# Small vector work handed from GpSimd to VectorE, and conditioning and cached values loaded at other places, in a two-layer diffusion step

## The chip, the cores and the metric

The kernel runs on one core of one Trainium2 chip. A core has TensorE (PE in the profile: matrix products and transposes, with PEld for its weight loads), VectorE (DVE), ScalarE (ACT), GpSimd (POOL) and SyncE (SP), which here issues nearly all DMAs. Each engine runs its own instructions in order and waits on the others by semaphores. The metric is the device time of one execution in microseconds (us): 1993.41, the median of three runs.

## The reference

One inference step of a backbone with two layers over 256 context tokens and 1024 latent tokens, model width 1024, all in float32. Layer 0 mixes tokens with differential attention (8 heads, two score maps of width 64 each, values of width 128), layer 1 with multi-head latent attention. Around both stands the same frame:

```python
sh, sc, gt = silu(cond) @ w_ada[i] + b_ada[i]            # conditioning, one vector for context, one for latent
h  = rmsnorm(x, g_pre[i]) * (1 + sc) + sh
x  = x + gt * rmsnorm(mixer(h) @ w_out[i], g_post[i])

# layer 0, differential attention
q, k, v, gate = split(h @ w_in)                          # q and k of latent tokens get a rotary embedding
p  = softmax(q k^T / 8)                                  # two maps per head; latent: 1024 keys and 256 cached
w  = p[0] - lam * p[1]
o  = rmsnorm(w @ v, g_sub) * (1 - lam_init)
y  = o * silu(gate)                                      # then y @ w_out
```

The outputs are both updated token streams and the layers' states (keys and values of layer 0, compressed latents and positional keys of layer 1).

## The kernel before

**Precision.** Float32 products are made of three products of a rounded type: each operand is split into a high part and the rest, a low part, and `mm3` (L324 to L329) adds high x high, high x low, low x high. So everything that goes into a product costs a cast (the high part) and a subtraction (the low part). For a weight, `weights` (L304 to L322) takes two 128-row blocks at a time: a DMA into a buffer "wst" (three of them turn round, `bufs=3`), ScalarE's cast into "wh", and the subtraction into "wl" on L320, which GpSimd does, or GpSimd and VectorE in turn where `lo_engs=self.LO` is given (output products, layer 1's projections).

**Tokens.** The 1280 tokens are handled as five pairs of 128-row tiles: latent pairs 0 to 3 and the context pair 4 (`CTXP`). `norm_pair` (L257) sums squares on ScalarE, forms the reciprocal root on GpSimd (`rstd`, L248: a scaling on L251, a power on L253), and scales x on VectorE. `norm_pair_to_hT` (L280) transposes x on TensorE; ScalarE applies scale and shift of the conditioning into "hfull" (L297), VectorE copies the high part, and VectorE or GpSimd by a fixed list subtracts the low part (L299).

**The start.** `constants` (L119) brings both conditioning vectors, the four norm gains and the biases of both layers (96 rows of 128) into one tile "rb", transposes it with the identity (L134) and forms silu of the conditioning. `run` (L1494 on) then loads in this order on SP's queue: first piece of w_ada, x of pair 0, first weights of V, x of pairs 1 to 3, the other pieces. In this stage the order on TensorE is the order of the code: conditioning sums, then 12 products of zeros with the identity (`WARM`), then the norms and products of V of head pair 0, pair by pair.

**Layer 0.** Work items of fixed order ("k0 q0 k1 q1 ..." and then "v1 a0 a1 v2 g0 ...": keys, queries, values, gates of a head pair, and conditioning sums) are chained: an item's weights are loaded before the item in front of it ends (`chain`, and `yield None` in an item). The first string fills 60 to 360 us. From 360 to 960 us the second is fed in small portions, by planned costs, between the attention of the 8 heads: scores, maximum (VectorE, L605), its combination (L613, L614) and the exponential (ScalarE, L617), the weighted difference of the two maps (L648 on VectorE, its factor on L643), its transposes and their splitting (L671 to L674), and `l0_values` (L678), which ends with the norm over a head's output y. There the squares are summed on ScalarE, the power and its combination with the softmax sum are formed on GpSimd, and y is scaled (L707); 40 such pairs of scalings in all. An item of values has the cached values of its head pair to split too, ahead of its second token pair (`l0_cached_v`, L509: a load into a staging buffer "s", then a split). Rows of q and k go out to DRAM and come back in another layout ("qsd", "ksd"), again by SP.

**From 960 us.** `y_chunk` (L743) loads 256 columns of y and of the gate, multiplies them on GpSimd (L757), transposes and splits. `out_items` (L929) multiplies by w_out and sums squares, `residual` (L976) adds x, and three queues of deferred work (`Later`, with the distances `HD`, `HE`, `ND` in steps) put late y chunks, norms and transposes of layer 1's input between the products. From 1200 us layer 1 runs, and from 1800 us its output product, with the same `residual` at the very end.

**What sets the order.** Apart from the hand-ordered stretch at the start, a scheduler orders each engine's instructions by the code's order and its own estimates; buffers turn round in pools of a fixed number.

## Time and profile before

| what | value |
|---|---|
| time, median of 3 runs | 1993.41 us (1992.21 to 1994.4) |
| time of the profiled execution | 1997.65 us |
| its span in the trace | 1995.8 us |
| mean granted clock of TensorE | 0.989 |
| TensorE busy | 1911.7 us, 96% of the span |
| VectorE busy | 1248.4 us, 63% |
| ScalarE busy | 963.9 us, 48% |
| GpSimd busy | 498.9 us, 25% |
| moved by DMA | 237.66 MB, 119 GB/s over the span |

The span runs from the first to the last recorded instruction; the execution's own time has 1.85 us more around it. Shares of busy time are means over stages with different limits, so a table by stage is the thing to read first, then what TensorE waits for. A row of a group names the line, the engine, the operation, output and inputs with their shape, the count, then busy microseconds and mean nanoseconds of one, and behind the second bar how long the engine stood before these instructions and what ended most of that.

### The profile page before, as it was taken

The numbers are of one execution on the slowest core, as the hardware profiler recorded it, in microseconds if no ns is written. First come the engines' busy times: TensorE is split into PE (matmuls) and PEld (weight loads), VectorE is DVE, ScalarE is ACT, GpSimd is POOL, SyncE is SP. The second block draws the span as 40 slices with busy tenths as digits, with TensorE's granted clock in tenths as the row PEclk, the third lists the DMA queues.
The fourth block names the chain that finished last, engine by engine and source line by source line (L and its number), as shares of the span: only waits on it lengthen the run. The fifth ranks groups of instructions, "written<-read, shape, count | busy, mean of one in ns | idle before, by whom it ended". The sixth has DMA issues, their size and how long they took to land.

```text
span 1995.8 us, 36154 instructions
## 1 busy us (share of the span) xinstructions
PE 1911.7 (96%) x13468; PEld 1721.9 (86%) x13468; DVE 1248.4 (63%) x2461; ACT 963.9 (48%) x2409; POOL 498.9 (25%) x693
## 2 busy tenths in 40 slices
PE   6999999999999999999998999999999999999998
PEld 5788888798989787988898999889899999998998
DVE  4644446788878786888427533446667767777413
ACT  4422123667666665666435533335445554455421
POOL 3354443213121212224334442100000000004214
PEclk9999999999999999999998999999999999999999
DMA  8555544544455454455624312442110111113412
GB/s 307 170 169 175 188 157 137 157 138 132 128 147 162 129 165 127 133 148 180 194 98 135 97 51 62 145 135 60 42 36 28 47 39 50 38 38 96 160 56 106
DMA packets 225009, 237.66 MB, mean 119 GB/s; under 512 B 25313, under 2 KB 192577, under 8 KB 224705
## 3 DMA queue, kind: packets, MB, share of 16 engines
q1 hardware_dynamic: 224672, 235.29, 38.3%
q8 instruction: 107, 1.75, 0.4%
q14 instruction: 70, 0.57, 0.1%
q10 hardware_dynamic: 160, 0.05, 0.0%
HBM read 160.48 MB, written 74.78 MB: 118 GB/s over the span
## 4 chain that ended last, share of the span: by engine, by line
PE 43%; DVE 5%; POOL 3%; ACT 2%; issue 2%; DMA 2%; SPq 0%; POOLq 0%; ACTq 0%; DVEq 0%
PE pj L327 7%; PE pj L329 7%; PE pj L328 7%; PE tp L671 3%; PE tp L327 3%; PE tp L328 3%; PE tp L329 3%; PE S L1280 1%; PE S L1281 1%; PE S L1278 1%; PE S L1279 1%; PE S L1277 1%; PE S L603 1%; DVE ptl L674 1%; DMA yst<-yTd 1%
## 5 line engine op out<-in xcount | busy, mean ns | idle before, releaser
L327 PE MATMUL pj<-wh,hh 128*128 128x256 f32 (+1 forms) x1264 | 369.4, 292 | 6.6 <-DVE ptl L674 3.5
L328 PE MATMUL pj<-wl,hh 128*128 128x256 f32 (+1 forms) x1264 | 359.1, 284 | 6.1 <-DVE wl L320 3.7
L329 PE MATMUL pj<-wh,hl 128*128 128x256 f32 (+1 forms) x1264 | 358.8, 284 | 3.4 <-POOL hl L299 1.7
L320 POOL TENSOR_TENSOR wl<-wst,wh 128x512 fp32r<-128x512 f32 (+3 forms) x95 | 110.7, 1173 | 655.1 <-ACT wh L319 608.9
L327 PEld LDWEIGHTS pj<-wh,hh 128*128 128x128 f32 x1264 | 241.7, 191 | 11.7 <-DVE ptl L674 4.1
L328 PEld LDWEIGHTS pj<-wl,hh 128*128 128x128 f32 x1264 | 242.2, 192 | 8.3 <-DVE wl L320 4.1
L329 PEld LDWEIGHTS pj<-wh,hl 128*128 128x128 f32 x1264 | 241.7, 191 | 6.5 <-POOL hl L299 3.1
L329 PE MATMUL pj<-hh,wl 128*128 128x512 f32 (+1 forms) x512 | 188.5, 368 | 1.0 <-POOL wl L365 0.9
L327 PE MATMUL pj<-hh,wh 128*128 128x512 f32 (+1 forms) x512 | 188.3, 368 | 0.0
L328 PE MATMUL pj<-hl,wh 128*128 128x512 f32 (+1 forms) x512 | 187.8, 367 | 0.0
L605 DVE TENSOR_REDUCE mA<-S 128x1 f32<-128x1024 f32 x128 | 155.4, 1219 | 46.8 <-PE S L603 45.9
L617 ACT ACTIVATE e<-S,bias 128x1024 f32<-128x1024 f32 x128 | 142.9, 1117 | 81.6 <-DVE bias L614 81.4
L603 PE MATMUL S<-kl,q 128*128 128x512 f32 x512 | 150.4, 414 | 5.5 <-ACT e L617 5.1
L673 ACT CAST pth<-tp 128x512 fp32r<-128x512 f32 (+1 forms) x208 | 98.4, 511 | 83.0 <-PE tp L671 81.9
L673 ACT CAST pth<-pj 128x512 fp32r<-128x512 f32 (+1 forms) x192 | 98.4, 519 | 73.4 <-PE pj L671 70.8
L674 DVE TENSOR_TENSOR ptl<-tp,pth 128x512 fp32r<-128x512 f32 (+1 forms) x208 | 115.1, 580 | 14.1 <-ACT pth L673 13.3
L648 DVE SCALAR_TENSOR_TENSOR e<-e,cf,e 128x512 f32<-128x512 f32 (+1 forms) x192 | 121.4, 674 | 1.1
L674 DVE TENSOR_TENSOR ptl<-pj,pth 128x512 fp32r<-128x512 f32 (+1 forms) x192 | 113.0, 592 | 12.1 <-ACT pth L673 11.5
L329 PEld LDWEIGHTS pj<-hh,wl 128*128 128x128 f32 x512 | 96.3, 188 | 20.9 <-POOL wl L365 3.9
L328 PEld LDWEIGHTS pj<-hl,wh 128*128 128x128 f32 x512 | 96.3, 188 | 16.9
L319 ACT CAST wh<-wst 128x512 fp32r<-128x512 f32 (+3 forms) x136 | 76.7, 574 | 70.1 <-issue 24.9
L603 PEld LDWEIGHTS S<-kl,q 128*128 128x128 f32 x512 | 88.8, 192 | 25.1 <-ACT e L617 8.1
(323 smaller groups left out, 5247.7 us busy)
## 6 DMA issues: line engine op xcount, KB each, us to landing
q<-qsd SPq DMA_DIRECT2D x320, 64.0 KB, 2.1
wst<-in_da_w_in_dram SPq DMA_DIRECT2D x64, 256.0 KB, 3.5
kl<-ksd SPq DMA_DIRECT2D x64, 192.0 KB, 3.7
wst<-in_w_out_dram SPq DMA_DIRECT2D x48, 256.0 KB, 2.9
ast<-in_w_ada_dram SPq DMA_DIRECT2D x8, 1024.0 KB, 6.3
wh<-in_w_ada_dram SPq DMA_DIRECT2D x32, 256.0 KB, 4.2
wl<-in_w_ada_dram SPq DMA_DIRECT2D x32, 256.0 KB, 5.1
vdh<-s SPq DMA_DIRECT2D x24, 256.0 KB, 2.1
```

Source lines behind the costliest of these rows:

```text
L319: nc.scalar.copy(wh, st)
L320: (lo_engs or [nc.gpsimd])[k0 // kb % len(lo_engs or [0])].tensor_tensor(out=wl, in0=st, in1=f32(wh), op=ALU.subtract)
L327: nc.tensor.matmul(out, a[0], b[0], start=first, stop=False)
L328: nc.tensor.matmul(out, a[0], b[1], start=False, stop=False)
L329: nc.tensor.matmul(out, a[1], b[0], start=False, stop=last)
L603: nc.tensor.matmul(S[:, so:so + 512], st(cc, o), kl[cc][:, so:so + 512], start=(o == 0), stop=(o == 1))
L605: nc.vector.reduce_max(out=mA[:, cc:cc + 1], in_=S, axis=AX.X)
L617: nc.scalar.activation(u.es[cc][:, 0:1024], A[cc], AF.Exp, bias=bias[:, cc:cc + 1], scale=0.125, accum_out=u.zA[:, cc:cc + 1])
L648: nc.vector.scalar_tensor_tensor(out=w[:, sl], in0=w[:, sl], scalar=cf, in1=e0[:, sl], op0=ALU.mult, op1=ALU.add)
L671: nc.tensor.transpose(tp[:, j, :], u.e[:, (c0 + j) * P:(c0 + j + 1) * P], self.ident)
L673: nc.scalar.copy(hi, tp[:, 0:cn, :])
L674: nc.vector.tensor_tensor(out=u.ptl[g][:, 0:cn, u.i * P:(u.i + 1) * P], in0=tp[:, 0:cn, :], in1=f32(hi), op=ALU.subtract)
```

## The change

Nothing of what is computed changes. Five things are done elsewhere or at another time:

1. **Low parts on VectorE.** `weights` always subtracts on VectorE (the list of engines is gone), and so does `norm_pair_to_hT`. The low parts that `weights_x` makes for keys and queries stay on GpSimd, as do the rotations there.
2. **Scalings and sums on VectorE.** The scaling in `rstd`, the sums of squares in `norm_pair` and `out_items`, the product of y and gate, and the additions of `residual`. The power of a reciprocal root stays on GpSimd. In `l0_values` the factor is no longer formed by itself: one instruction scales y by both factors.
3. **Conditioning in a tile of its own.** The two conditioning vectors come into a tile "rc" of 16 rows and are transposed alone; gains and biases come into "rb" of 80 rows, which is transposed behind the conditioning sums, in `ada_bias`.
4. **Order at the start.** The DMA of pair 0's x goes ahead of the first piece of w_ada. Of the 12 products of zeros, 8 stand ahead of the conditioning sums and 4 behind.
5. **Cached values with the weights.** They are loaded by the item's `load`, into one of the three "wst" buffers, ahead of the item's four weight pieces; the split stays where it was.

GpSimd's instructions fall from 698 to 266, VectorE's rise from 2463 to 2816, TensorE's from 13294 to 13295.

```diff
-    WARM = 12
+    WARM = 8
...
     def constants(self, cp, tmp, ps):
         nc, I = self.nc, self.I
-        rb = self.t(tmp, [96, P], "rb")
-        vecs = [I["c"][0], I["c_ctx"], I["g_pre"][0], I["g_pre"][1], I["g_post"][0], I["g_post"][1]]
+        rc = self.t(tmp, [16, P], "rc")
+        for i, v in enumerate([I["c"][0], I["c_ctx"]]):
+            nc.scalar.dma_start(rc[8 * i:8 * i + 8, :], v.rearrange("(a p) -> a p", p=P))
+        rb = self.t(tmp, [80, P], "rb")
+        vecs = [I["g_pre"][0], I["g_pre"][1], I["g_post"][0], I["g_post"][1]]
...
-        nc.tensor.transpose(pt[:, 0:96], rb, self.ident[:96, :96])
-        self.cols = self.t(cp, [P, 12, 8], "cols")
-        nc.vector.tensor_copy(self.cols, pt[:, 0:96].rearrange("p (a b) -> p a b", b=8))
+        nc.tensor.transpose(pt[:, 0:16], rc, self.ident[:16, :16])
+        ccol = self.t(cp, [P, 2, 8], "ccol")
+        nc.vector.tensor_copy(ccol, pt[:, 0:16].rearrange("p (a b) -> p a b", b=8))
...
-    def ada_bias(self, pool):
+    def ada_bias(self, cp, pool):
         nc = self.nc
+        pt = self.t(self.c.pj, [P, 512], "pj")
+        nc.tensor.transpose(pt[:, 0:80], self.rb, self.ident[:80, :80])
+        self.cols = self.t(cp, [P, 10, 8], "cols")
+        nc.vector.tensor_copy(self.cols, pt[:, 0:80].rearrange("p (a b) -> p a b", b=8))
...
     def rstd(self, pool, ss, n, width=1, tag="rs"):
-        nc.gpsimd.tensor_scalar(out=v, in0=ss, scalar1=1.0 / n, scalar2=EPS, op0=ALU.mult, op1=ALU.add)
+        nc.vector.tensor_scalar(out=v, in0=ss, scalar1=1.0 / n, scalar2=EPS, op0=ALU.mult, op1=ALU.add)
...
-            nc.gpsimd.tensor_tensor(out=ss[:, 0, :], in0=ss[:, 0, :], in1=ss[:, 1, :], op=ALU.add)
+            nc.vector.tensor_tensor(out=ss[:, 0, :], in0=ss[:, 0, :], in1=ss[:, 1, :], op=ALU.add)
...
-                (nc.vector if k in (self.HL if l else (1, 3, 5, 7)) else nc.gpsimd).tensor_tensor(out=hl[:, k, :], in0=full, in1=f32(hh[:, k, :]),
-                                                              op=ALU.subtract)
+                nc.vector.tensor_tensor(out=hl[:, k, :], in0=full, in1=f32(hh[:, k, :]), op=ALU.subtract)
...
             nc.scalar.copy(wh, st)
-            (lo_engs or [nc.gpsimd])[k0 // kb % len(lo_engs or [0])].tensor_tensor(out=wl, in0=st, in1=f32(wh), op=ALU.subtract)
+            nc.vector.tensor_tensor(out=wl, in0=st, in1=f32(wh), op=ALU.subtract)
...
+        def load():
+            cr = self.l0_load_cached_v(hp) if kind == "v" else None
+            return self.weights(W, [((2048 if kind == "v" else 3072) + hp * 256, 256)]), cr
+
+        def gen(ld):
+            ws, cr = ld
...
                 if kind == "v" and pr == 1:
-                    self.l0_cached_v(hp)
+                    self.l0_split_v(hp, cr, 8)
...
-    def l0_cached_v(self, hp):
-        cr = self.t(self.c.stg, [P, 2, 256], "s")
+    def l0_load_cached_v(self, hp):
+        cr = self.t(self.wp, [P, 2, 256], "wst", bufs=3)
         self.nc.sync.dma_start(cr, self.I["cache_diff_v"][0, 0, :, 2 * hp:2 * hp + 2].rearrange(
             "(t p) h d -> p t (h d)", p=P))
-        self.l0_split_v(hp, cr, 8)
+        return cr
...
         r = self.rstd(c.st, ss, P, 2, tag="ors")
         for i in range(2):
-            f = self.t(c.st, [P, 1], "of")
-            nc.gpsimd.tensor_tensor(out=f, in0=r[:, i:i + 1], in1=rz[i], op=ALU.mult)
-            nc.gpsimd.tensor_scalar(out=y[:, i, :], in0=y[:, i, :], scalar1=f, scalar2=None, op0=ALU.mult)
+            nc.vector.tensor_scalar(out=y[:, i, :], in0=y[:, i, :], scalar1=r[:, i:i + 1], scalar2=rz[i],
+                                    op0=ALU.mult, op1=ALU.mult)
...
-        nc.gpsimd.tensor_tensor(out=y, in0=y, in1=g, op=ALU.mult)
+        nc.vector.tensor_tensor(out=y, in0=y, in1=g, op=ALU.mult)
...
-            nc.gpsimd.tensor_tensor(out=xt[:, i, :], in0=xt[:, i, :], in1=tmp, op=ALU.add)
+            nc.vector.tensor_tensor(out=xt[:, i, :], in0=xt[:, i, :], in1=tmp, op=ALU.add)
...
-                nc.gpsimd.tensor_tensor(out=z[:, i, :], in0=z[:, i, :], in1=x0[i], op=ALU.add)
+                nc.vector.tensor_tensor(out=z[:, i, :], in0=z[:, i, :], in1=x0[i], op=ALU.add)
...
+            load_x(0)
             load_ada(0)
-            self.ada_bias(self.ac)
-            load_x(0)
             load_v(0)
...
             load_x(4)
+            cached = self.l0_load_cached_v(0)
             with tc.manual_schedule(engines={mybir.EngineType.PE}):
-                m = ada_sums(0)
                 idle = self.t(ps, [P, 512], "xt")
                 for _ in range(self.WARM):
                     nc.tensor.matmul(idle, self.identr, self.zeros, start=True, stop=True)
+                m = ada_sums(0)
+                for _ in range(self.WARM // 2):
+                    nc.tensor.matmul(idle, self.identr, self.zeros, start=True, stop=True)
+                self.ada_bias(cp, self.ac)
                 ada_cols(0, m)
```

The scheduler puts the moved instructions at new places. Each row below has the line, the operation, output and inputs (with the numbers of their buffers) and the shape; line numbers behind the change are up to 13 higher.

The first place is VectorE at the very start: "identr" is the identity that every transpose and the products of zeros need, "ss" and "rsv" belong to the norm of the first x. Before:

```order
L129 CAST identr_227<-idt_222 128x128
L147 TENSOR_REDUCE sel_242<-idt_222 128x2
L136 COPY cols_233<-pj_231 128x96
L140 TENSOR_SCALAR cc_237<-cols_233 128x16
L181 COPY bias_141_254<-cols_233 128x48
L183 TENSOR_SCALAR bias_141_254<-cols_233 128x8 x2
L144 SCALAR_TENSOR_TENSOR silc_239<-th_235,cc_237 128x2x8
L270 TENSOR_SCALAR x_258<-x_258,rs_363 128x1024
```

With the change:

```order
L258 TENSOR_SCALAR rsv_368<-ss_363 128x2
L131 CAST identr_228<-idt_223 128x128
L149 TENSOR_REDUCE sel_243<-idt_223 128x2
L138 COPY ccol_234<-pj_232 128x16
L277 TENSOR_SCALAR x_251<-x_251,rs_370 128x1024
L142 TENSOR_SCALAR cc_238<-ccol_234 128x16
L277 TENSOR_SCALAR x_252<-x_252,rs_370 128x1024
L146 SCALAR_TENSOR_TENSOR silc_240<-th_236,cc_238 128x2x8
L326 TENSOR_TENSOR wl_260<-wst_261,wh_259 128x512
L1479 COPY m_173_341<-ad_324 128x512
```

The scaling of the first norm's sum (rsv) now stands ahead of the identity's cast, and a low part of V's weights (L326) ahead of the copy of the conditioning sums (L1479).

The second place is the norm over y in layer 0's attention ("oss" and "ors" are its sum and its power, "ptl" the low part of transposed weights). Before, on GpSimd, behind three low parts of the item's weights:

```order
L320 TENSOR_TENSOR wl_3036<-wst_3037,wh_3035 128x512
L320 TENSOR_TENSOR wl_3042<-wst_3043,wh_3041 128x512
L320 TENSOR_TENSOR wl_3048<-wst_3049,wh_3047 128x512
L251 TENSOR_SCALAR orsv_3663<-oss_3576 128x2
L253 TENSOR_TENSOR ors_3665<-orsv_3663,mhalf_229 128x2
L706 TENSOR_TENSOR of_3667<-ors_3665,rz_3307 128x1
L706 TENSOR_TENSOR of_3670<-ors_3665,rz_3423 128x1
L707 TENSOR_SCALAR y_3575<-y_3575,of_3667 128x128
L707 TENSOR_SCALAR y_3575<-y_3575,of_3670 128x128
```

With the change, on VectorE, behind one of the first heads' units:

```order
L624 TENSOR_TENSOR m_4458<-m_4458,mA_4461 128x2
L654 SCALAR_TENSOR_TENSOR cf_4527<-Z_4339,neglam_1091,rz_4525 128x1
L625 SCALAR_TENSOR_TENSOR bias_4459<-m_4458,negl_1097 128x2
L258 TENSOR_SCALAR orsv_4534<-oss_4437 128x2
L659 SCALAR_TENSOR_TENSOR e_4377<-e_4377,cf_4527,e_4376 128x512 x2
L659 SCALAR_TENSOR_TENSOR e_4377<-e_4377,cf_4527,e_4376 128x256
L716 TENSOR_SCALAR y_4436<-y_4436,ors_4536,rz_4159 128x128
L716 TENSOR_SCALAR y_4436<-y_4436,ors_4536,rz_4282 128x128
L616 TENSOR_REDUCE mA_4583<-S_4585 128x1
L685 TENSOR_TENSOR ptl_934_4455<-pj_4591,pth_931_4452 128x4x128
```

The sum's scaling (L258) and y's (L716) now stand between the bias and the weighted difference of one unit and the maxima of another; GpSimd's power, not in this row, lies between the two.

The third place is SP's queue where the weights of the first item of values ("v1") are loaded, while the last queries are still being written. Before:

```order
L457 DMA out_dram<-s_2859 128x2x256
L317 DMA wst_3031<-in_da_w_in_dram 128x2x256
L388 DMA ksd_116_184<-hi_2882 128x256
L388 DMA ksd_116_184<-lo_2883 128x256
L388 DMA ksd_116_184<-hi_2888 128x256
L388 DMA ksd_116_184<-lo_2889 128x256
L317 DMA wst_3037<-in_da_w_in_dram 128x2x256
L317 DMA wst_3043<-in_da_w_in_dram 128x2x256
L317 DMA wst_3049<-in_da_w_in_dram 128x2x256
L388 DMA qsd_112_180<-hi_2943 128x512
L388 DMA qsd_112_180<-lo_2944 128x512
```

With the change:

```order
L463 DMA out_dram<-s_2864 128x2x256
L522 DMA wst_3034<-in_cache_diff_v_dram 128x2x256
L394 DMA ksd_116_184<-hi_2887 128x256
L394 DMA ksd_116_184<-lo_2888 128x256
L394 DMA ksd_116_184<-hi_2893 128x256
L394 DMA ksd_116_184<-lo_2894 128x256
L323 DMA wst_3038<-in_da_w_in_dram 128x2x256
L323 DMA wst_3044<-in_da_w_in_dram 128x2x256
L323 DMA wst_3050<-in_da_w_in_dram 128x2x256
L394 DMA qsd_112_180<-hi_2948 128x512
L394 DMA qsd_112_180<-lo_2949 128x512
```

The cached values (L522) have the place of the item's first weight piece. The other three take the places of the three behind it, and the fourth piece, wst_3056, stands nine rows behind wst_3050, past all eight qsd writes of 128x512, where before it had gone out ahead of them.

37 lines of the change are left out of this document (18 added, 19 removed).

## The prediction

> **What bounds the kernel now.** I read the page's busy times first, then a table of busy time by stage, then what TensorE waits for, then the groups of GpSimd and VectorE, whose work changes hands.
>
> ```profile
> PE 1911.7 (96%) x13468; PEld 1721.9 (86%) x13468; DVE 1248.4 (63%) x2461; ACT 963.9 (48%) x2409; POOL 498.9 (25%) x693
> ```
>
> TensorE is busy for 96% of the span, so at most 84 us could ever be won by taking waits away, and VectorE has 37% free on average. The average hides the stages; the next table has one row each, with the columns PE, PEld, DVE, ACT, POOL, granted clock, DMA share and GB/s.
>
> ```profile
> 0.00:60.00 60.00, 43.17 (x345) 34.80 (x349) 30.18 (x66) 27.04 (x51) 21.21 (x37) 0.94 0.76 260
> 200.00:360.00 160.00, 156.11 (x895) 134.68 (x896) 87.51 (x135) 46.83 (x106) 61.94 (x55) 0.99 0.48 156
> 360.00:780.00 420.00, 408.41 (x2910) 355.64 (x2909) 332.34 (x662) 271.26 (x716) 94.84 (x178) 0.99 0.50 146
> 780.00:960.00 180.00, 170.91 (x1264) 154.51 (x1264) 157.71 (x299) 123.17 (x314) 56.48 (x88) 0.99 0.54 160
> 960.00:1040.00 80.00, 76.71 (x622) 73.46 (x623) 21.65 (x32) 30.23 (x84) 25.41 (x35) 0.98 0.35 113
> 1040.00:1200.00 160.00, 142.71 (x1168) 139.54 (x1167) 88.55 (x169) 75.15 (x197) 72.59 (x117) 0.96 0.33 101
> 1200.00:1800.00 600.00, 596.00 (x4093) 541.46 (x4092) 380.11 (x831) 278.27 (x653) 39.11 (x49) 1.00 0.20 60
> ```
>
> Three places matter. In the opening 60 us TensorE stands 17 us. In 1040 to 1200 (the end of layer 0's output product, norms, first products of layer 1) it stands 17 us. In 780 to 960 (the last heads of layer 0) VectorE is busy 157.7 of 180 us, 88%: the one stage where it has next to no room. From 1200 to 1800 TensorE stands 4 us in 600, and nothing can be won.
>
> ```profile
> PE pj L134 <- DMA ast<-in_w_ada_dram: 9.9, 1, 9.9
> PE xt L290 <- ACT hfull L297: 9.8, 5, 3.4
> PE pj L328 <- DVE wl L320: 3.7, 2, 3.3
> PE pj L768 <- POOL xt L757: 3.3, 1, 3.3
> ```
>
> The first wait is the start. The second and third lie between 1040 and 1200, behind residuals and norms. The fourth is GpSimd's multiplication of a late y chunk, just before 1000.
>
> **The change, part by part.** What moves, and what VectorE asks for the like:
>
> ```profile
> L320 POOL TENSOR_TENSOR wl<-wst,wh 128x512 fp32r<-128x512 f32 x71 | 94.0, 1331 | 228.9 <-ACT wh L319 184.5 <-PE tp L671 44.1 <-DMA wst<-in_da_w_in_dram 0.4
> L707 POOL TENSOR_SCALAR y<-y,of 128x128 f32<-128x128 f32 x80 | 51.5, 656 | 0.0
> L253 POOL TENSOR_TENSOR ors<-orsv,mhalf 128x2 f32<-128x2 f32 x40 | 29.0, 724 | 3.3
> L674 DVE TENSOR_TENSOR ptl<-tp,pth 128x512 fp32r<-128x512 f32 x128 | 85.0, 683 | 11.8 <-ACT pth L673 11.0
> L320 DVE TENSOR_TENSOR wl<-wst,wh 128x512 fp32r<-128x512 f32 x37 | 32.1, 872 | 25.4 <-ACT wh L319 25.4
> L1302 DVE TENSOR_SCALAR e<-e,rz 128x256 f32<-128x256 f32 x16 | 6.3, 393 | 0.5
> L614 DVE SCALAR_TENSOR_TENSOR bias<-m,negl 128x2 f32<-128x2 f32 x64 | 14.2, 221 | 0.2
> L613 DVE TENSOR_TENSOR m<-m,mA 128x2 f32<-128x2 f32 x64 | 13.9, 218 | 0.1
> L643 DVE SCALAR_TENSOR_TENSOR cf<-Z,neglam,rz 128x1 f32<-128x1 f32 x64 | 17.8, 279 | 1.1 <-DVE rz L641 0.2
> ```
>
> A low part of 128x512 costs GpSimd 1.33 us; VectorE took 0.87 us where GpSimd ran beside it, and 0.68 us for the same shape out of PSUM (L674). I take 0.68 us, since GpSimd falls silent beside most of them. The scaling of y (128x128, two factors from tiles) has no row on VectorE: it costs between the 0.15 us of its smallest instructions (the second row below) and 0.39 us for twice the width (L1302); I take 0.33, nearer that row. What GpSimd does to VectorE meanwhile:
>
> ```profile
> 839.18 1.22 DVE L614 SCALAR_TENSOR_TENSOR bias<-m,negl 128x2 f32<-128x2 f32 x1
> 851.69 0.15 DVE L614 SCALAR_TENSOR_TENSOR bias<-m,negl 128x2 f32<-128x2 f32 x1
> 837.84 2.55 POOL L320 TENSOR_TENSOR wl<-wst,wh 128x512 fp32r<-128x512 f32 x2 [4.67 <-ACT wh L319]
> ```
>
> The same 128x2 instruction takes 0.15 us alone and 1.22 us while GpSimd subtracts a weight; it ends when GpSimd does, at 840.4. Every score's exponential waits for it. So moving a subtraction adds 0.68 us and takes away up to 1.3 us of standing.
>
> **Layer 0's attention, 360 to 960.** Counts of L320 (DVE, POOL), L707 and L757 (POOL) in the two stages:
>
> ```profile
> 360.00:780.00 420.00, 0.00 (x0) 25.78 (x20) 0.99 0.50 146
> 780.00:960.00 180.00, 0.00 (x0) 5.14 (x4) 0.99 0.54 160
> 360.00:780.00 420.00, 33.76 (x52) 0.99 0.50 146
> 780.00:960.00 180.00, 14.14 (x22) 0.99 0.54 160
> 780.00:960.00 180.00, 22.81 (x17) 0.99 0.54 160
> 820.00:840.00 20.00, 20.00 (x164) 19.46 (x163) 18.67 (x38) 12.24 (x33) 5.35 (x8) 1.00 0.37 110
> ```
>
> In 780 to 960 VectorE gets 22 scalings at 0.33 and 11 sums of 0.15 (8.9 us), 4 subtractions (2.7) and 17 products of y and gate (11.6): 23.2 us. It loses the standing: at least 5 us (L614, L613 and L643 stand 0.07, 0.07 and 0.13 us above the 0.15 of one alone, 64 times each, 17 us in 600, and the stage is 180 of them), at most all 28 us of GpSimd's subtractions and products there. I take 12, since GpSimd's time is shared between contended and idle moments. 157.7 + 23.2 - 12 is 168.9 us. The busiest slice shows that VectorE reaches 18.67 of 20, 93%; 168.9 / 0.93 is 181.6: **+2 us**. With 5 us of relief it is 189, +9; with 28 it would be short of VectorE's limit and half of TensorE's 9 us of standing could go, -5. In 360 to 780 the same sum is 332.3 + 26 x 0.81 + 20 x 0.68 - 9 = 358 of 420, 85%: no change, cover by TensorE's 408 of 420. The y scaling now stands in VectorE's own row behind GpSimd's power (0.72 us) and ScalarE's squares. Where the order puts one to five other instructions between, as it mostly does, the power is covered; queued behind it are the maxima and ptl that TensorE waits for, and uncovered it costs 0.72 us each.
>
> [...]
>
> **Weights with the cached values.** The cached tile takes one of three "wst" buffers ahead of the item's four weight pieces, so the fourth piece of v1 is issued behind eight qsd writes.
>
> ```profile
> 315.43 0.39 PE L328 MATMUL pj<-wl,hh 128*128 128x256 f32 x1 [0.84 <-POOL wl L320]
> wst<-in_da_w_in_dram SPq DMA_DIRECT2D x64, 256.0 KB, 3.5
> qsd<-hi SPq DMA_DIRECT2D x16, 256.0 KB, 2.0
> ```
>
> Before, v1 waits 0.8 us for a low part. Now the piece leaves when the rotated q is out, needs 3.5 us to land, a cast and 0.68 us, some 5 us behind that, while TensorE has 8 score products (3 us) to put ahead: **+2 us**, between 0 (the order covers it) and +5.
>
> **The start.** In the trace the conditioning's rows land last:
>
> ```profile
> 9.85 0.39 PE L134 MATMUL pj<-identr,rb 96*128 96x96 f32 x1 [9.85 <-DMA ast<-in_w_ada_dram]
> 20.20 1.02 ACT L297 ACTIVATE hfull<-xt,ada 128x256 f32<-128x256 f32 x2 [2.66 <-PE xt L290]
> GB/s 0 160 379 257 348 383 382 398 427 407 421 404 402 360 348 350 347 377 355 346 348 312 48 130 384 357 351 367 430 374 126 120 0 0 5 0 0 3 172 11
> ```
>
> Slices are 1.5 us; 160 + 379 + 257 GB/s put 1.05 MB (the first x) down by 5.5 us and the 2.1 MB of w_ada behind it by 10.5. [...] hfull comes at 18, 2 us sooner, but the next pairs' scaling stands behind both low parts on VectorE, and gives one back: **-1 us**, between -3 and +2.
>
> **960 to 1200.** The late y product falls from 1.3 to 0.68 us and GpSimd's queue ahead of it (scalings, low parts) is gone: of the 3.3 us wait **-3**, between -5 and 0. Between residual and norm each pair loses two additions on GpSimd, such as this one,
>
> ```profile
> 1990.58 1.43 POOL L989 TENSOR_TENSOR x<-x,ztmp 128x256 f32<-128x256 f32 x1 [0.60 <-DVE ztmp L987]
> ```
>
> for VectorE's, half of 0.68 us plus a little, 0.4: 2 us a pair sooner. TensorE's five waits of 1.96 us on average can each lose 1.2: **-6**, between -12 (the 9.8 and 3.7 us of the rows above nearly gone) and +3 (all low parts now stand behind z on VectorE, and the 3.3 us wait comes twice). **Rest:** the last addition is on the tail, -1, between -1.5 and +0.5; low parts waited for in 200 to 360, -1; 1200 to 1900 0, between -3 and +4, hidden by TensorE's 596 of 600.
>
> **Sum:** +2 +2 -1 -3 -6 -1 -1 = -8 us. The profiled execution took 1997.65 us (span 1995.8 and 1.85 around it), 4.2 above the median 1993.41. 1997.65 - 8 = 1989.65, and 4.2 less for the median: **1986 us** rounded up, -0.4%.
>
> **The rivals.**
> *VectorE becomes the bound (slower).* Place: 360 to 960. Relief at its 5 us end (+9), and half of the 37 y pairs find the power uncovered, 37 x 0.72 / 2 = 13 us. With the other terms (-10) that is +12, 2005 us. It decides once VectorE's row passes 93% in 780 to 960. For it: 88% already, and ScalarE, VectorE, GpSimd, VectorE in one in-order row. Against: instructions between in most places. Chance 0.18.
> *The cached load starves the weights (slower).* v1's 5 us, and as much at two later items: 15 - 10 + 2 = +7, 2000 us. Against: later loads have attention work beside them. Chance 0.06.
> *Nothing moves.* TensorE at 96% hides it and gains and losses cancel: 1993 us, within 4. Chance 0.22.
> *The lock.* All standing goes: half of TensorE's 21 us in 360 to 960, 12 in 1040 to 1200, 3 and 1 around: -26, 1967 us. Against: 17 us is all that three small lines show above their shortest. Chance 0.11.
> *The forecast,* 1979 to 1990: 0.43.
>
> **How the numbers follow.** No change is within 0.2%, 4 us, about what a measurement of this kernel can tell. Faster: 0.39 of the forecast, 0.11 of the lock, 0.03 of nothing: 0.53. Same: 0.04 + 0.16 = 0.20. Slower: 0.18 + 0.06 + 0.03 = 0.27. The range 1969 to 2003 leaves out half of the lock and most of the first rival.
>
> **What would show it.** After: VectorE near 1330 us busy and GpSimd near 210; L614's like at 0.15 us throughout; in 780 to 960 VectorE at 93%, the stage no longer than 184; the five hfull waits below 5 us; the first hfull near 18 us; a wait of 2 us at v1's fourth piece. It is wrong if the attention grows by over 10 us or the waits of 1040 to 1200 stay.

## The result, and the profile after

The changed kernel takes 1972.04 us (1969.21 to 1976.34) where the kernel before took 1993.41: a ratio of 0.9888, with a 95% interval of 0.987 to 0.9907. Forecast were 1986, 0.4% less; it became 1.1% less, inside the range and the forecast way, but 14 us beyond the forecast and outside the 1979 to 1990 that the prediction gave its own mechanism. The profiled execution took 1976.34 us, its span is 1974.6, against 1995.8 before. Its page begins:

```profile
PE 1903.2 (96%) x13469; PEld 1720.5 (87%) x13469; DVE 1292.8 (65%) x2814; ACT 964.7 (49%) x2409; POOL 218.2 (11%) x261
```

GpSimd lost 281 us of work and VectorE gained only 44. The stages, in the columns of the prediction's table (PE, PEld, DVE, ACT, POOL, granted clock, DMA share, GB/s):

```profile
0.00:60.00 60.00, 45.04 (x355) 35.90 (x356) 31.19 (x91) 27.54 (x51) 6.80 (x16) 0.94 0.77 264
200.00:360.00 160.00, 156.24 (x899) 135.78 (x897) 86.08 (x143) 47.34 (x107) 51.22 (x44) 0.98 0.46 152
360.00:780.00 420.00, 407.71 (x2937) 358.34 (x2936) 352.23 (x771) 274.96 (x724) 21.91 (x27) 1.00 0.50 147
780.00:960.00 180.00, 171.12 (x1280) 153.73 (x1279) 165.12 (x352) 122.37 (x313) 8.69 (x11) 1.00 0.54 160
1040.00:1200.00 160.00, 153.77 (x1276) 149.74 (x1275) 94.71 (x239) 81.41 (x207) 26.86 (x58) 0.99 0.30 91
1200.00:1800.00 600.00, 595.49 (x4083) 541.87 (x4082) 389.80 (x883) 278.36 (x657) 11.43 (x13) 1.00 0.21 63
```

In 1040 to 1200 TensorE now stands 6 us where it stood 17. But the work has moved against the clock face, so a stage must be cut by what happens in it and not by the time. The next table cuts each trace at the same landmarks: the first product of the k0 item, the first and last score product of layer 0, the first transpose of layer 1's input, its first key-value transpose, the first and last score of layer 1.

| stage, us | before | after | difference |
|---|---|---|---|
| start, to the first product of k0 | 81.3 | 80.0 | -1.3 |
| key and query items | 236.9 | 234.9 | -2.0 |
| layer 0's attention, first score to last | 627.4 | 618.8 | -8.6 |
| to the first transpose for layer 1 | 109.7 | 108.2 | -1.5 |
| norms, to the first key-value transpose | 86.8 | 79.2 | -7.6 |
| rest of layer 1's projections | 213.5 | 211.7 | -1.8 |
| layer 1's attention | 498.9 | 501.0 | +2.0 |
| tail | 141.3 | 140.9 | -0.5 |

Two stages carry 16 of the 21 us. The two stages behind layer 0's attention, before and then after, by the landmarks:

```profile
945.52:1055.19 109.67, 102.29 (x806) 94.79 (x805) 44.15 (x75) 47.72 (x130) 38.16 (x51) 0.95 0.46 149
1055.19:1142.03 86.84, 76.45 (x614) 74.21 (x612) 59.07 (x113) 47.67 (x123) 40.97 (x52) 0.96 0.36 112
```

```profile
933.63:1041.85 108.22, 99.44 (x809) 92.68 (x808) 54.87 (x115) 47.33 (x130) 4.79 (x7) 0.98 0.49 159
1041.85:1121.05 79.20, 74.37 (x614) 72.55 (x613) 60.60 (x161) 48.66 (x124) 6.00 (x9) 0.98 0.40 129
```

In the stage of the norms TensorE stands 4.8 us where it stood 10.4. In both stages together the standing falls by only 4.2 of the 9.1 us (17.8 to 13.6); the granted clock, 0.95 and 0.96 before and 0.98 after, makes 4.1 more (half clock while TensorE is busy costs 7.5 us before and 3.4 after, summed over the stretches at 0.50). What TensorE waits for, in the view of waits:

```profile
PE pj L136 <- DVE identr L131: 7.4, 1, 7.4
PE pj L333 <- DVE ptl L685: 6.7, 11, 1.4
PE xt L297 <- ACT hfull L304: 4.7, 4, 2.7
PE pj L334 <- DVE wl L326: 4.4, 3, 2.1
PE pj L778 <- DVE xt L767: 2.4, 1, 2.4
```

The wait for hfull has halved (9.8 to 4.7 us); the late y product costs 2.4 us where it cost 3.3; the 2.1 us at a low part is v1's fourth weight piece. On VectorE, in the groups by shape (busy us, mean ns of one):

```profile
L624 DVE TENSOR_TENSOR m<-m,mA 128x2 f32<-128x2 f32 x64 | 9.7, 152 | 0.1
L625 DVE SCALAR_TENSOR_TENSOR bias<-m,negl 128x2 f32<-128x2 f32 x64 | 9.9, 155 | 0.1
L654 DVE SCALAR_TENSOR_TENSOR cf<-Z,neglam,rz 128x1 f32<-128x1 f32 x64 | 13.8, 216 | 1.0
L326 DVE TENSOR_TENSOR wl<-wst,wh 128x512 fp32r<-128x512 f32 x108 | 73.4, 688 | 45.1 <-ACT wh L325 44.2
L716 DVE TENSOR_SCALAR y<-y,ors,rz 128x128 f32<-128x128 f32 x64 | 19.7, 344 | 12.3 <-POOL ors L260 12.3
L767 DVE TENSOR_TENSOR wst<-wst,wst 128x512 f32<-128x512 f32 x7 | 4.8, 684 | 0.8 <-DMA wst<-g 0.8
```

The prices taken were right to a few hundredths: 0.69 us for a low part (0.68 taken), 0.34 for a scaling of y (0.33 taken), and the two 128x2 lines are at 0.15 us (the line of the factor, L654, is at 0.22, so its 0.28 before were 0.06 too long and not 0.13). Over the whole attention, by the landmarks, the two rows are, before and then after:

```profile
318.14:945.52 627.38, 605.20 (x4351) 537.17 (x4351) 509.37 (x996) 406.83 (x1065) 149.12 (x267) 0.99 0.50 147
```

```profile
314.87:933.63 618.76, 599.75 (x4348) 536.07 (x4348) 527.77 (x1143) 406.98 (x1065) 30.61 (x38) 0.99 0.50 146
```

The instructions that VectorE took over there last 54.3 us (low parts 16.7, scalings of y 23.4, products with the gate 8.1, sums 6.2), yet its busy time grew by 18.4. The other 36 us have two sources. The lines that were on VectorE before last some 20 us less than they did: six of them make 19 of it (by the groups 4.2 at m, 4.3 at the bias, 4.0 and 1.1 at the two factors, 3.5 and 2.1 at the two differences of the maps). That is the standing that went away, against 12 and 9 us forecast for most of this stretch. The rest, some 15 us, is no standing: the record of an instruction on VectorE begins on average 0.06 us (before) and 0.07 us (after) before the record ahead of it ends, so that the 996 instructions of before last 569.4 us for 509.4 busy, and the 1143 of after 605.3 for 527.8. TensorE stands 3.2 us less in this stage (22.2 before, 19.0 after), and its busy time is 5.4 us shorter.

### The profile page after: what moved, and what is told of

Same layout as the page of the kernel before. It is cut to its first block, busy times and chain, and to the rows that moved or that the text cites. A ratio compares the mean times of both kernels' runs of the same rounds, so it can differ in the third digit from the quotient of the medians.

```text
span 1974.6 us, 35965 instructions
## 1 busy us (share of the span) xinstructions
PE 1903.2 (96%) x13469; PEld 1720.5 (87%) x13469; DVE 1292.8 (65%) x2814; ACT 964.7 (49%) x2409; POOL 218.2 (11%) x261
## 4 chain that ended last, share of the span: by engine, by line
PE 80%; DVE 11%; ACT 3%; issue 2%; POOL 2%; DMA 2%; ACTq 0%; SPq 0%; POOLq 0%; DVEq 0%
PE pj L333 16%; PE pj L335 16%; PE pj L334 15%; PE S L614 5%; PE tp L682 3%; PE tp L333 3%; PE tp L334 3%; PE tp L335 3%; PE pj L682 2%; DVE mA L616 2%; DVE ptl L685 2%; PE S L1288 1%; PE S L1290 1%; PE S L1291 1%; PE S L1289 1%
## 5 line engine op out<-in xcount | busy, mean ns | idle before, releaser
L333 PE MATMUL pj<-wh,hh 128*128 128x256 f32 (+1 forms) x1264 | 368.2, 291 | 10.5 <-DVE ptl L685 6.0
L614 PE MATMUL S<-kl,q 128*128 128x512 f32 x512 | 150.5, 413 | 1.4 <-ACT e L628 0.9
L684 ACT CAST pth<-tp 128x512 fp32r<-128x512 f32 (+1 forms) x208 | 98.2, 511 | 80.9 <-PE tp L682 79.9
L326 DVE TENSOR_TENSOR wl<-wst,wh 128x512 fp32r<-128x512 f32 (+3 forms) x136 | 84.3, 629 | 52.8 <-ACT wh L325 51.9
L325 ACT CAST wh<-wst 128x512 fp32r<-128x512 f32 (+3 forms) x136 | 76.9, 575 | 73.8 <-PE pj L334 21.7
L333 PEld LDWEIGHTS pj<-hh,wh 128*128 128x128 f32 x512 | 96.3, 188 | 16.6
```

What stands on the lines that cost most here:

```text
L325: nc.scalar.copy(wh, st)
L326: nc.vector.tensor_tensor(out=wl, in0=st, in1=f32(wh), op=ALU.subtract)
L333: nc.tensor.matmul(out, a[0], b[0], start=first, stop=False)
L614: nc.tensor.matmul(S[:, so:so + 512], st(cc, o), kl[cc][:, so:so + 512], start=(o == 0), stop=(o == 1))
L684: nc.scalar.copy(hi, tp[:, 0:cn, :])
```

## The experiments

Each row of the table is one profiled execution, cut at the landmarks; executions of one kernel differ by a few us (up to 11 in E7), so the time beside it is the median with the ratio to the kernel before. One stretch at half clock moves a stage by 1.7 or 3.4 us (last section), so a difference of 2 or 3 us in a stage, from one execution each, is not clear of that. The first four columns behind the time are those stages that move.

| kernel | time, ratio [95%] | key/query | attention | norms | l. 1 projections |
|---|---|---|---|---|---|
| before | 1993.4 | 236.9 | 627.4 | 86.8 | 213.5 |
| after | 1972.0, 0.9888 [0.987, 0.9907] | 234.9 | 618.8 | 79.2 | 211.7 |
| E1 after, GpSimd busy again | 2003.3, 1.0045 [1.003, 1.006] | 234.8 | 624.9 | 89.8 | 222.5 |
| E2 after, VectorE busier | 1986.9, 0.9958 [0.9941, 0.9974] | 234.7 | 626.2 | 81.1 | 216.4 |
| E3 after, y back | 1986.3, 0.9952 [0.9936, 0.9968] | 234.6 | 632.9 | 78.4 | 211.7 |
| E4 after, weights' low parts back | 1979.4, 0.9922 [0.9907, 0.9938] | 234.4 | 621.7 | 79.9 | 213.6 |
| E5 as E3, y written by GpSimd | 1982.4, 0.9934 [0.9921, 0.9948] | 234.3 | 628.6 | 79.2 | 211.7 |
| E6 after, y written by GpSimd | 1985.6, 0.9953 [0.994, 0.9966] | 234.4 | 631.1 | 79.3 | 211.8 |
| E7 before, y written by GpSimd | 1993.1, 0.9993 [0.9982, 1.0004] | 235.4 | 626.9 | 88.8 | 213.5 |
| E8 after, hl back | 1975.9, 0.9901 [0.9887, 0.9914] | 233.5 | 617.8 | 82.0 | 211.8 |
| E9 after, other order | 1968.5, 0.9874 [0.9854, 0.9894] | 234.4 | 615.7 | 79.2 | 211.6 |
| E10 before, other order | 2001.5, 1.004 [1.0025, 1.0056] | 236.4 | 625.3 | 86.4 | 215.1 |
| E11 before, y alone on VectorE | 1999.6, 1.0025 [1.0014, 1.0036] | 236.8 | 629.5 | 88.5 | 213.4 |
| E12 after, residual and products back | 1988.9, 0.9969 [0.9957, 0.9981] | 234.5 | 623.1 | 82.6 | 211.7 |

**E1: GpSimd as busy as before, and nobody waiting for it.**

```diff
             nc.vector.tensor_tensor(out=wl, in0=st, in1=f32(wh), op=ALU.subtract)
+            nc.gpsimd.tensor_tensor(out=st, in0=st, in1=f32(wh), op=ALU.subtract)
```

> The changed kernel, and beside every low part that VectorE now makes of a weight GpSimd makes the same difference once more, into the staging buffer itself, which nobody reads after that. TensorE waits for none of it; GpSimd is busy again and holds the staging buffer as it did before the change. Theory 'standing' (VectorE's instructions stand while GpSimd subtracts, and that is what the attention paid before): the 128x2 line of the bias, 155 ns in the changed kernel, goes back above 200 ns, the attention (618.8 us from the first score to the last in the changed kernel) becomes 4 to 8 us longer, and the whole 5 to 12 us, 1977 to 1984. Theory 'hops' (the gain is that fewer results pass through GpSimd, and standing costs nothing): the bias line rises too, but the time stays within 3 us of 1972.

It became 31 us slower than the changed kernel, more than twice the most that either theory gave (12). The bias line rose only from 155 to 181 ns, where over 200 was expected, and the attention, 6 us longer, is the smaller part: 11 us each came in the norms and in layer 1's projections, where nothing of this was expected. The first row is SP's wait for the staging buffers in the changed kernel, the others are E1's: that wait, one of TensorE's, and GpSimd's row at that place.

```profile
SPq L323 <- DVE wl L326: 181.3, 52, 30.3
```

```profile
SPq L323 <- POOL wst L327: 292.3, 92, 30.5
...
PE tp L1089 <- POOL kps L1083: 3.7, 1, 3.7
```

```profile
1180.89 4.69 POOL L327 TENSOR_TENSOR wst<-wst,wh 128x512 f32<-128x512 f32 x3 [1.74 <-DVE wl L326]
1187.66 1.26 POOL L327 TENSOR_TENSOR wst<-wst,wh 128x512 f32<-128x512 f32 x1
1189.21 0.45 POOL L1083 TENSOR_TENSOR kps<-kpe,kps 128x128 fp32r<-128x128 f32 x1 [0.29 <-DVE kps L1082]
```

The extra differences hold the three staging buffers longer, so the next pieces are loaded later; and they stand in GpSimd's in-order row ahead of the rotation and the copy of layer 1's positional keys, for which TensorE then waits 3.7 us. So this run is no clean measure of standing. It shows what an unread result on a quiet engine can cost by its buffer and by its place in the row.

**E2: VectorE made busier.**

```diff
             nc.vector.tensor_tensor(out=wl, in0=st, in1=f32(wh), op=ALU.subtract)
+            nc.vector.tensor_tensor(out=st, in0=st, in1=f32(wh), op=ALU.subtract)
```

> The changed kernel, and VectorE makes every low part of a weight twice, the second time into the staging buffer: 136 more instructions, 93 us of VectorE, about 17 of them in the attention. If VectorE bounds the end of the attention, as the forecast's +2 us assumed (it decides from 93% busy in the last 180 us), the attention becomes 5 to 17 us longer and the time 1977 to 1990. If VectorE has room there, the attention stays within 3 us of 618.8, and the time within 4 us of 1972; in the start and between 1040 and 1120, where TensorE waits for low parts, up to 3 us may be lost either way.

In the attention VectorE's busy time rose by 16 us (527.8 to 543.9) and the stage by 7.5: in this run 1 us more of VectorE goes with 0.46 us of the stage. The whole is 15 us slower. Both lie in what the forecast's term had expected (5 to 17 and 1977 to 1990). But the price is not shown as VectorE's alone: the extra differences hold the staging buffers too (SP waits 191 us for them, 181 in the changed kernel), and they reorder the rows. The stage got shorter with the change all the same.

**E3 and E4: one part taken back.** E3 gives the norm over y back to GpSimd, E4 the weights' low parts.

```diff
-        r = self.rstd(c.st, ss, P, 2, tag="ors")
+        r = self.rstd(c.st, ss, P, 2, tag="ors", eng=nc.gpsimd)
         for i in range(2):
-            nc.vector.tensor_scalar(out=y[:, i, :], in0=y[:, i, :], scalar1=r[:, i:i + 1], scalar2=rz[i],
-                                    op0=ALU.mult, op1=ALU.mult)
+            f = self.t(c.st, [P, 1], "of")
+            nc.gpsimd.tensor_tensor(out=f, in0=r[:, i:i + 1], in1=rz[i], op=ALU.mult)
+            nc.gpsimd.tensor_scalar(out=y[:, i, :], in0=y[:, i, :], scalar1=f, scalar2=None, op0=ALU.mult)
```

> The changed kernel with only the norm over y given back to GpSimd (scaling of the sum, the factor, and both scalings of y: 160 instructions). Rival 'VectorE becomes the bound': y's scaling stands in VectorE's row behind GpSimd's power, so giving it back makes the kernel faster, by 5 to 13 us, 1959 to 1967. Theory 'hops' or 'standing': GpSimd is nearly idle now, so its 0.7 us a scaling costs little by itself; the time stays within 3 us, or up to 5 us slower by what these scalings (51 us of GpSimd) hold up of VectorE.

```diff
-            nc.vector.tensor_tensor(out=wl, in0=st, in1=f32(wh), op=ALU.subtract)
+            (lo_engs or [nc.gpsimd])[k0 // kb % len(lo_engs or [0])].tensor_tensor(out=wl, in0=st, in1=f32(wh), op=ALU.subtract)
```

> The changed kernel with only the weights' low parts given back to the engines that made them before (98 on GpSimd, the others in turn). Theory 'standing' and theory 'hops' both have it slower: 'standing' by 4 to 8 us in the attention and 2 to 4 us elsewhere, 1978 to 1984, about as much as the extra differences on GpSimd cost; 'hops' by 2 to 5 us, in single waits of TensorE for such a low part and with the attention as it is, 1974 to 1977.

E3 came out against both expectations: 14 us slower, all of it in the attention. So the rival by which y's scaling blocks VectorE's row is refuted for the changed kernel: there the scalings stand 12.3 us in all behind GpSimd's power, and having them is worth more. E4 is 7 us slower, as theory "standing" had it (1978 to 1984), but the attention shows 2.9 of it, less than the 4 to 8 expected, and the projections of layer 1 show 1.9. Where E3 loses is seen when its matmuls are counted against the changed kernel's: it falls 6 us behind up to 720 us (waits of 1.7 us at 651 and 2.1 at 663, with half clock behind both), another 4 between 754 and 766, and another 4 between 780 and 790 (a wait of 2.2 us for ScalarE's copy of y and one of 1.0). The place at 754, E3's SP queue and TensorE:

```profile
745.02 2.78 SPq L572 DMA_DIRECT2D q<-qsd  x6
754.20 0.38 SPq L719 DMA_DIRECT2D y<-y  x1
754.68 0.41 SPq L205 DMA_DIRECT2D wh<-in_w_ada_dram  x1
758.03 1.03 PE L196 MATMUL pj<-wh,silc 128*32 128x512 f32 x1 [2.23 <-DMA wh<-in_w_ada_dram]
```

SP stands from 747.8 to 754.2 at the write of a y that is not ready; the conditioning weights are queued behind it, and TensorE waits for them. The kernel before has the very same place. Its SP queue, TensorE, and the windows of 2 us:

```profile
739.20 2.79 SPq L561 DMA_DIRECT2D q<-qsd  x6
748.37 0.38 SPq L708 DMA_DIRECT2D y<-y  x1
748.85 0.42 SPq L198 DMA_DIRECT2D wh<-in_w_ada_dram  x1
752.53 1.03 PE L189 MATMUL pj<-wh,silc 128*32 128x512 f32 x1 [2.55 <-DMA wh<-in_w_ada_dram]
```

```profile
750.00:752.00 2.00, 0.00 (x0) 0.00 (x0) 1.37 (x3) 0.00 (x0) 0.00 (x0) 0.71 0.89 244
752.00:754.00 2.00, 1.47 (x4) 0.36 (x4) 0.00 (x0) 0.00 (x0) 0.00 (x0) 0.50 1.04 350
754.00:756.00 2.00, 2.00 (x8) 1.10 (x6) 0.00 (x0) 0.00 (x0) 0.00 (x0) 0.50 1.03 373
756.00:758.00 2.00, 2.00 (x9) 1.19 (x7) 1.17 (x2) 1.68 (x4) 0.00 (x0) 0.58 0.54 206
```

Six us of SP's standing become 2.6 us of TensorE's, and the granted clock (the third number from the end) then stays at half for some 7 us more. Counted by matmuls, the kernel before falls back 5.4 us against the changed one in this place alone. It had been 3.5 us ahead of it until then; 3 more are lost between 840 and 860 and the rest around 940, where TensorE waits 2.7 us for the exponential and is at half clock behind it. In the changed kernel the write stands behind those loads, and SP stands 112 us at the 40 writes of y in all, against 180 before (from the end of the issue ahead to the write's own). It is not that y comes earlier: from ScalarE's copy to the scaled y it takes 6.5 us on average after, 4.8 before. The write has only got another place in the row.

**E5, E6 and E7: y's write out of SP's queue.** The one line, on E3, on the changed kernel and on the kernel before:

```diff
-        nc.sync.dma_start(self.ydram[pr].rearrange("(t p) n -> p t n", p=P)[:, :, h * P:(h + 1) * P], y)
+        nc.gpsimd.dma_start(self.ydram[pr].rearrange("(t p) n -> p t n", p=P)[:, :, h * P:(h + 1) * P], y)
```

> The run before with the norm over y on GpSimd, and now y's write to DRAM is issued by GpSimd instead of standing in SP's queue. Theory 'queue' (SP's in-order queue stands at y's write, 184 us in 40 writes there against 112 us in the changed kernel, and the loads behind it come late): with the write gone from SP's queue the 14 us that giving the norm back had cost come back, the attention returns from 632.9 to 614 to 622 us, the time to 1970 to 1976. Theory 'order' (what matters is the order in which the scheduler put TensorE's work, or the engine on which y is scaled): it stays at 1983 to 1990.

> The changed kernel with only the write of y issued by GpSimd, which waits there for VectorE's scaling. Theory 'queue': SP stands no more for 112 us in 40 writes; what of it TensorE still pays in the attention comes off, so 1964 to 1972. Theory 'order': 1970 to 1975, no change.

> The kernel before with only the write of y issued by GpSimd, so that all vector work is where it was. Theory 'queue': most of what the change won in the attention comes from this alone: the attention falls from 627.4 to 614 to 620 us and the time by 7 to 14 us, 1980 to 1987, and TensorE's wait of 2.6 us for the conditioning weights at 750 us, with the half clock behind it, is gone. Theory 'standing' (VectorE held up by GpSimd) and 'order': within 3 us of 1993.5.

E5 wins back 4 of 14 us. E7 loses the step at 750 us as foreseen (by the count of matmuls it is 0.8 us ahead there, where the kernel before falls 5.4 behind the changed one), but gives the gain away at 680 and 830 us, and the whole is the same. E6 is 13 us slower. Two rows tell of part of E6's loss, the wait and the time from issue to landing:

```profile
PE pj L622 <- ACT y L708: 5.6, 3, 3.4
y<-y POOLq DMA_DIRECT2D x40, 128.0 KB, 2.8
```

From SP's queue the same write landed in 1.9 us in the changed kernel. y has one buffer; ScalarE's copy of the next y waits until the write has landed (1.95 us in E11's row below), and behind ScalarE TensorE stands, 5.6 us in all in E6. So the free queue was no cure here, with a later landing and a single buffer. Theory "queue" holds for the step that the rows show, and falls as the account of the whole stage.

**E8 and E12: what the stage of the norms had paid.**

```diff
-                nc.vector.tensor_tensor(out=hl[:, k, :], in0=full, in1=f32(hh[:, k, :]), op=ALU.subtract)
+                (nc.vector if k in (self.HL if l else (1, 3, 5, 7)) else nc.gpsimd).tensor_tensor(out=hl[:, k, :], in0=full, in1=f32(hh[:, k, :]), op=ALU.subtract)
```

> The changed kernel with only the low parts of the transposed norms (50 of 80 on VectorE before, the others on GpSimd) given back as before. Forecast's step: the gain of 6 us between 1040 and 1140 is the residual additions', so this costs at most 2 us in that stage. Rival: the gain is that ScalarE no longer waits for GpSimd's low part to free a buffer of hfull (3.1 to 3.3 us each of several times before); then the stage from the first transposes of layer 1 to the first of its key values (79.2 us in the changed kernel) becomes 4 to 8 us longer, the start 1 to 3 us, and the time 1976 to 1982.

```diff
-        nc.vector.tensor_tensor(out=y, in0=y, in1=g, op=ALU.mult)
+        nc.gpsimd.tensor_tensor(out=y, in0=y, in1=g, op=ALU.mult)
...
-            nc.vector.tensor_tensor(out=xt[:, i, :], in0=xt[:, i, :], in1=tmp, op=ALU.add)
+            nc.gpsimd.tensor_tensor(out=xt[:, i, :], in0=xt[:, i, :], in1=tmp, op=ALU.add)
...
-                nc.vector.tensor_tensor(out=z[:, i, :], in0=z[:, i, :], in1=x0[i], op=ALU.add)
+                nc.gpsimd.tensor_tensor(out=z[:, i, :], in0=z[:, i, :], in1=x0[i], op=ALU.add)
...
-            nc.vector.tensor_tensor(out=ss[:, 0, :], in0=ss[:, 0, :], in1=ss[:, 1, :], op=ALU.add)
+            nc.gpsimd.tensor_tensor(out=ss[:, 0, :], in0=ss[:, 0, :], in1=ss[:, 1, :], op=ALU.add)
```

(and the sums of squares in the output items)

> The changed kernel with the product of y and gate, the residual additions and the sums of squares given back to GpSimd, low parts left on VectorE. The forecast's step (these additions delay each pair by 2 us, the late product by 3): the stretch from the attention's end to the first key values of layer 1 (187.4 us in the changed kernel) becomes 4 to 7 us longer, the tail 1 us, the time 1977 to 1981. As the low parts given back took 3 us of that stretch's 9, the rest, about 6, should be here. Rival (GpSimd, idle but for these, is quick enough): under 3 us.

In the stage of the norms E8 costs 2.8 us, E12 3.4 and E4 0.7: together 6.9 of the 7.6 won. So neither the forecast's step nor the rival had it alone. Of E8's 2.8 us 1.7 are one more stretch at half clock. E12 loses another 2.3 us in the stage ahead; the 5.7 of both are in the 4 to 7 that the forecast's step had given it, and its rival (under 3) is refuted. E12 moves three things at once, and which of them counts was not separated. The low parts' share is seen in the kernel before, on ScalarE and on GpSimd, as the two buffers of hfull are given free:

```profile
1060.87 0.77 POOL L299 TENSOR_TENSOR hl<-hfull,hh 128x256 fp32r<-128x256 f32 x1
1061.67 1.02 ACT L297 ACTIVATE hfull<-xt,ada 128x256 f32<-128x256 f32 x2 [3.16 <-POOL hl L299]
```

E12's whole, 17 us by the medians, is more than its stages show in the profile (4.3 in the attention, 3.4 in the norms, 2.3 ahead of them). The two profiled executions differ by only 7.7 us: E12's lies with 1984 us 5 below its median, at a granted clock of 0.990 where the median of its twelve is 0.988, and the changed kernel's lies 4 above its own. The rest thus lies between executions of one kernel.

**E9, E10 and E11: the order alone, and y alone.** E9 and E10 cut the planned portions of the attention otherwise, on the changed kernel and on the kernel before; E11 moves only the norm over y.

```diff
-    FEV, FOD, FX = (0.4, 0.4, 0.6, 1.0, 2.0, 0.4), (0.1, 0.1, 0.2, 0.3, 0.3, 0.1), (0.0, 0.0, 1.0, 1.6, 0.5, 0.6)
+    FEV, FOD, FX = (0.5, 0.5, 0.6, 1.0, 1.8, 0.4), (0.1, 0.1, 0.2, 0.3, 0.3, 0.1), (0.0, 0.0, 1.0, 1.6, 0.5, 0.6)
```

> The changed kernel with the same instructions on the same engines; only the planned portions that the attention hands to the other products are cut differently (0.5, 0.5, 0.6, 1.0, 1.8, 0.4 for 0.4, 0.4, 0.6, 1.0, 2.0, 0.4), which moves about 4% of TensorE's instructions, as many as the change itself had moved. Theory 'order' (the attention's gain is what this order happens to give, whichever engine scales y): the attention, 618.8 us, moves by 4 to 12 us, more likely up, the time to 1974 to 1984. Theory 'y' (VectorE's scaling of y itself is worth 8 to 14 us): it stays within 3 us, 1969 to 1975.

> The kernel before with the same other portions and nothing else. Theory 'order': the attention, 627.4 us, moves by 4 to 12 us to either side, the time to 1982 to 2004 and not near 1993. Theory 'y': within 3 us, 1990 to 1996.

```diff
-            f = self.t(c.st, [P, 1], "of")
-            nc.gpsimd.tensor_tensor(out=f, in0=r[:, i:i + 1], in1=rz[i], op=ALU.mult)
-            nc.gpsimd.tensor_scalar(out=y[:, i, :], in0=y[:, i, :], scalar1=f, scalar2=None, op0=ALU.mult)
+            nc.vector.tensor_scalar(out=y[:, i, :], in0=y[:, i, :], scalar1=r[:, i:i + 1], scalar2=rz[i],
+                                    op0=ALU.mult, op1=ALU.mult)
```

> The kernel before with only the norm over y on VectorE (the scaling of its sum, and one scaling of y by both factors). Theory 'y': as giving it back had cost 14 us in the attention, doing it alone wins 8 to 14 us there, time 1979 to 1986. Theory 'order': the order is another one once more, and the attention lands anywhere between 615 and 635 us, the time between 1982 and 2001; a gain of under 5 us speaks for it.

The same work in another order is 3.6 us faster on the changed kernel (the shortest time of all here, though the intervals of the two ratios overlap) and 7 us slower on the kernel before (1.004, interval clear of 1); the attention itself moves by -3.1 and -2.1, less than the 4 to 12 expected, the rest lies around it. So this one other order counts for some 3 to 7 us, and theory "order" holds only in part; other orders were not tried.

E11 decides against theory "y": what cost 14 us when taken back from the changed kernel costs 5 us when put into the kernel before. There y's scaling on VectorE stands behind GpSimd's power for 17.5 us in all instead of 12.3; most of the difference is two places, 3.1 us at 932, where two products of y and gate stand ahead of the power on GpSimd, and 1.4 at 962, where a weight's low part does. SP stands 117 us at the writes of y in E11, as in the changed kernel (112), and the loss at 750 us is gone; the stage is 2 us longer than before all the same. E11's waits at one place, ScalarE and TensorE, and then TensorE of the changed kernel there:

```profile
382.40 0.37 ACT L697 COPY y<-pj 128x256 f32<-128x256 f32 x1 [1.95 <-DMA y<-y]
382.83 1.06 PE L189 MATMUL pj<-wh,silc 128*32 128x512 f32 x1 [2.78 <-ACT y L697]
```

```profile
381.92 0.62 PE L196 MATMUL pj<-wh,silc 128*32 128x512 f32 x1 [1.59 <-ACT y L708]
```

The y of the unit before is late, its one buffer is still being written out, ScalarE cannot copy the next, and TensorE stands 2.8 us. GpSimd is not what delays it here, for it is idle ahead of the power: the scaling of y's sum stands in VectorE's row until 5.0 us after ScalarE's copy begins (1.4 us in the kernel before, on GpSimd). The changed kernel has the same place and waits 1.6 us in it, with 3.4 us at half clock behind where E11 has 6.8. So the rival of the prediction, y in a row of ScalarE, VectorE, GpSimd, VectorE, is seen in both, and it costs E11 more.

## Why the prediction was right, and where it was not

**Direction and size.** It went the forecast way and stayed in the range, at 21 us where 8 were summed. It lies in the range by the part that was left for "the lock", not by the forecast's own 1979 to 1990, and that part is luck: the lock's sum is not what the runs show (below). Nearly all of the difference to the forecast is one term, the attention. VectorE ended at 1293 us busy (1330 forecast), GpSimd at 218 (210).

**Layer 0's attention, +2: wrong, -8.6 measured.** The step that failed is "157.7 + 23.2 - 12, over 93%", in two ways. The standing taken away was sized well: some 20 us over the whole attention against the 21 taken. Mis-sized was what the moved instructions add: 58 us were taken for 360 to 960, but as neighbouring records overlap, the 54 us that they last made VectorE busy for only some 40 more. So VectorE stayed at 165 of 180 where 169 were forecast, and the same division by 93% would have given 177.5, no loss. And the limit at 93% was the only thing looked at. A busier VectorE does go with a longer stage (E2: 0.46 us for each us, not cleared of the staging buffers), but the largest single place that the stage had been paying lay elsewhere, in SP's row: one write of y, ahead of loads that TensorE was waiting for, with a clock at half behind it, 5.4 us. The view of SP's waits had shown it:

```profile
SPq L708 <- POOL y L707: 128.9, 38, 5.7
```

The prediction looked at the queues only for the start and for v1; the scaling of y was costed with VectorE's row and not with the DMA behind it.

**What of the attention stays open.** What made the stage 8.6 us shorter as a whole is not shown. The place at 750 us is not enough: E7 and E11 are both free of it and their attention is no shorter than before (626.9 and 629.5 against 627.4). The parts don't add. Taken back one by one they cost 14.1 (y), 2.9 (weights), 4.3 (products and residual) and -1.0 (low parts of the norms) in the attention, 20 us against the 8.6 won; y put in alone costs 2. The sign of E11 is explained only in part, by y's one buffer at 382 us and the power's wait at 932. Each of these edits also reorders TensorE's row in this stage, and order alone moved the whole by 4 to 7 us; which share of E3's 14 us is order and which is y on GpSimd was not separated. Some 6 of these 14 are half clock (10.5 us of it while TensorE is busy, 4.8 in the changed kernel), behind waits at other places than the changed kernel's. A second buffer for y was not tried.

**The start, -1: -1.3 measured, and not to be told from nothing.** Kernels with the old start took 81.3, 79.2, 81.1 and 79.1 us to k0's first product, kernels with the new one 79.2 to 81.2. In the trace the sum for x's norm (7.08 us) stands ahead of the identity's cast and the zeros wait for the power until 8.7, and the conditioning's sums behind the first eight of them begin at 12.4. The 18 us of hfull, from which the -1 is taken, was the author's estimate and stands in no row of before; with the change hfull came at 17.6. By the rates of the prediction's own row the 2.1 MB behind the first x end near 11 us, not at 10.5.

**Weights with the cached values, +2: the wait came, the cost did not.** TensorE waits 2.1 us at v1's fourth piece, as forecast, where it waited twice 0.8 before. But the stage of the key and query items became 2 us shorter. The cause of those 2 us is open: E4, E8 and E12 keep them, and the cached load was not tried alone. Half clock follows the wait (at 314 us), but it followed the two short ones before as well (at 317).

**960 to 1200, -9: -9.1 measured** (1.5 and 7.6), right in the sum by luck and wrong in the split. The sum was of waits, but the waits gave only 4.2 us; 4.1 came from the clock, which the prediction left out. The late product gave 0.9 of the 3 forecast. Of the norms' 7.6 us 3.4 came back with E12 (products, residual and sums together, not the residual's additions alone, for which 6 were forecast); 2.8 came back with E8, the low parts by which GpSimd held the buffers of hfull, and the prediction had these only as a danger on VectorE.

**Rest, -2: -2.2 measured** (in rounded parts: key and query items -2.0, layer 1's projections -1.8, of which E4 gives the weights' low parts 1.9, its attention +2.0, tail -0.5). Layer 1's attention has 3.4 us more of half clock, behind waits of under 2 us.

**The rivals.** "The lock" gave 1967 us, the nearest of all numbers to 1972. That VectorE's 128x2 lines stood beside a busy GpSimd is seen: L614's 221 ns became 155 as GpSimd's busy time in the attention fell from 149.1 to 30.6 us, 181 with E1's differences. Its size is not: that all 28 us of GpSimd's work from 780 to 960 come off as relief was the author's estimate, which no run shows, and over the whole attention some 20 went. Its account of the gain was not right either: it took half of TensorE's standing from 360 to 960 for VectorE's, but TensorE's standing in the attention fell by 3.2 us, and E4 puts 13 us of VectorE's standing back and loses 2.9 in this stage. "VectorE becomes the bound" did not come: its condition was over 93% in 780 to 960, and VectorE has 92% in the changed kernel (165.1 us) and 89% in E11 (159.6), which was slower without it; only E2, with its extra differences, reaches 93% (167.6). "The cached load starves the weights" did not come either, and its sum has v1's own 2 us in it twice: 15 - 10 gives +5, 1998 us, not +7.

## What to carry to other kernels

An edit that changes when a result is ready can move the DMA that writes it, and with it everything queued behind that DMA: read the waits of the DMA queue's engine with the same care as those of the compute engines. Parts that share an in-order row and a single buffer need not add: here one part alone was slower than nothing, and the same part taken out again cost 14 us. Busy time that went up by less than the work moved is not all standing won: compare the lines that stayed, one by one. Where a scheduler orders the work, run the same work in a second order before a difference of a few us is given a cause.
